# Weight maxima turned on VectorE before they go to memory, in a one-core hybrid attention layer

## The chip, the cores and the metric

The kernel runs on one core of one Trainium2 chip. The metric is the device time of one execution in microseconds (us). The core has five engines with instruction streams of their own: TensorE (PE in the profile, with PEld for its weight loads), VectorE (DVE), ScalarE (ACT), GpSimd (POOL) and SyncE (SP). SP and POOL also issue DMA transfers, each from its own queue, and all transfers share the core's 16 DMA engines.

## The reference

One decoder layer of 2048 tokens with 1024 features, depth 1. A modulated, normalised input goes through one wide projection; two mixers work on it (causal "forgetting" attention with 8 heads, and sliding-window attention with 8 query heads on 2 key heads); each mixer's output is gated, both go through one output projection, a norm and a residual.

```python
mod = jax.nn.silu(c) @ w_ada[l] + b_ada[l]
shift, scale, gate = jnp.split(mod, 3, axis=-1)
h = rms_norm(x, g_pre[l]) * (1.0 + scale[:, None, :]) + shift[:, None, :]
proj = h @ w_in[l]
qa, ka, va, fa, za, qb, kb, vb, zb = jnp.split(proj, split_points, axis=-1)
oa = forgetting_attention(qa, ka, va, fa + b_fgate[l])      # heads of 64
oa = oa * jax.nn.silu(za)
ob = sliding_window_sink_attention(rope(qb), rope(kb), vb, sinks[l])
ob = ob * jax.nn.silu(zb)
y = jnp.concatenate([oa, ob], axis=-1) @ w_out[l]
x = x + gate[:, None, :] * rms_norm(y, g_post[l])
```

## The kernel before

**Numbers in two halves.** Every large product is made of 16-bit matmuls: an operand is scaled by a power of two and split into a high and a low fp16 half, and three of the four products of halves are summed. For weights the power of two comes from the largest absolute value of a block of 128 columns (a "key": `kb`, `vb`, `qb0`-`qb3`, `zb0`-`zb3`, `va0`-`va3`, `za0`-`za3`, `qk0`-`qk7`; a `qk` key holds a head's 64 query and 64 key columns of the forgetting attention).

**How a key's weights are made ready.** For all but the first three keys, eight steps stand as events at fixed distances ahead of the key's first matmul, counted in units of projection work (42, 31, 21, 12, 8, 6, 4 and 3 units ahead):

1. `w_load` (L204): POOL issues the load of the block, 128 partitions x 8 x 128 numbers.
2. `w_max` (L210): VectorE reduces it to one largest absolute value on each partition, 128x1. Its `put` (L215) has POOL write these 128 numbers to a small tensor in memory, `mx_d` (three of them in turn). In the projection and sliding-window stage `put` follows at once; in the forgetting-attention stage it is held back for four ticks of the order (`lag`).
3. `w_back` (L225): POOL issues a read of the 512 bytes that spreads all 128 numbers over every partition (`mxr`, 128x128). It has to wait until `mx_d` has landed.
4. `w_scale` (L236 on): VectorE reduces `mxr` along the row, so that every partition knows the largest of all, and makes the power of two and its inverse in four small instructions (five for `qk` keys).
5. `w_high` (L251, ScalarE) and `w_low` (L257, VectorE, two parts) make the halves; `w_done` makes the factors for later scalings.

The keys `kb`, `vb` and `zb0` take their maxima in the first stage through TensorE instead and don't use `mx_d`.

**Stages and order.** The order of instructions is written out by hand: a list of projection units is worked off (`fill`), and between them stand the events, delayed pieces of work (`after`, `tick`) and the attention steps. In the first stage the modulation is computed and the input is normalised and turned (`hT`); then come projections mixed with rotary work (`evac_rope`: SP copies `qf` to `qs` with halves exchanged, POOL multiplies by the sines at L717, VectorE adds at L718); then, from about 140 us on, windows of the sliding attention (`Pair`) with projections between; from about 446 us the forgetting attention. `gates` (from L773) computes the logarithms of the forget gates: VectorE L782 joins them and TensorE sums them at L787 and L788.

In the forgetting attention each head's q and k come out of TensorE at L313, are split (`evac_qk`, ScalarE L1002 and VectorE L994) and copied by five SP transfers (L997 to L1000) into the tile `T`, where they stand twice in different arrangements. `max_units` (TensorE L1213, VectorE L1216 and L1218) reads `T` to find row maxima of scores. A `Step` computes scores into `sta` (L1262, L1263), exponentials (ScalarE L1267), a causal mask (POOL L1271), high and low halves (ScalarE L1275, VectorE L1278) and the product with the values (L1288, L1290, L1291) in `poa`. At the end of a row block VectorE divides (`ona`, L1295 and L1297), and the next block may use `poa` again. SP stores `ona` to memory; in the last stage the outputs are gated, turned and multiplied with the output weights (L1413).

POOL's queue holds, in order, weight loads (L204), writes and read backs of maxima, gate stores (`z_d`, L361), the rotary multiplication (L717), output stores of the sliding windows (L897), copies of sinks (L848) and the causal mask (L1271). All of them are worked off in the order in which they were issued, also when the first in line waits.

Of the kernel before, what the change touches and what calls it, by code (L numbers as in the profile page):

```python
# [10 lines left out]
F32 = mybir.dt.float32  # L11
# [4 lines left out]
ALU = mybir.AluOpType  # L16
AX = mybir.AxisListType

P = 128
# [21 lines left out]
def hybrid_layer(  # L41
# [17 lines left out]
    V, A, G, PE, SP = nc.vector, nc.scalar, nc.gpsimd, nc.tensor, nc.sync  # L59
# [12 lines left out]
    const = ctx.enter_context(tc.tile_pool(name="const", bufs=1))  # L72
# [4 lines left out]
    mx_d = [dram.tile([P, 1], F32, name=f"mx_d{n}") for n in range(3)]  # L77


    def sm(n, tag):  # L80
        return small.tile([P, n], F32, tag=tag, name=tag)
# [51 lines left out]
    cosT = swc.tile([P, S], F32, name="cosT")  # L133
    sinT = swc.tile([P, S], F32, name="sinT")
    pH = const.tile([P, 1], F32, name="pH")
    Gp = const.tile([P, KT], F32, name="Gp")
    Shp = const.tile([P, KT], F32, name="Shp")

# [46 lines left out]
    def after(n, f):  # L185
        late.append([n, f])
# [8 lines left out]
    wq = {}  # L195
    kaps_seen = []
# [9 lines left out]
        wq[key] = [raw]  # L206

    def w_max(key):
        mx = sm(1, "w_mx")
        V.tensor_reduce(mx[:], wq[key][0][:], axis=AX.XY, op=ALU.max, apply_absolute_value=True)  # L210
        md = mx_d[len(kaps_seen) % 3]
        kaps_seen.append(key)

        def put():
            G.dma_start(md[:], mx[:])  # L215
            wq[key].append(md)

        if lag[0]:
            after(lag[0], put)
        else:  # L220
            put()
# [684 lines left out]
    def add(key, us):  # L906
        if key not in pkeys and key not in ("kb", "vb"):
            at = len(punits) - (24 if key[:2] == "za" else 0)
            for n, (lead, f) in enumerate(((42, lambda: w_load(key, pieces(key))), (31, lambda: w_max(key)),
                                           (21, lambda: w_back(key)), (12, lambda: w_scale(key)),  # L910
                                           (8, lambda: w_high(key)), (6, lambda: w_low(key, 0)),
                                           (4, lambda: w_low(key, 1)), (3, lambda: w_done(key)))):
                if key == "zb0":
                    if n >= 3:
                        events.setdefault(n + 9, []).append(f)
                else:
                    events.setdefault(max(at - lead, n), []).append(f)
        if key not in pkeys:
            pkeys.append(key)
        punits.extend(us)  # L920
# [3 lines left out]
    for kind, j in (("zb", 0), ("zb", 1), ("va", 0), ("zb", 2), ("zb", 3), ("va", 1), ("va", 2)):  # L924
        key = f"{kind}{j}"
# [549 lines left out]
    with tc.manual_schedule():  # L1475
# [28 lines left out]
        for s, stp_ in enumerate(steps):  # L1504
            hd, r = divmod(s, NS)
# [100 lines left out]
```

## Time and profile before

| | |
|---|---|
| median of 3 runs | 1215.64 us (1214.23 to 1216.64) |
| profiled execution | 1216.32 us; its span, first to last instruction, 1214.5 us |
| mean granted TensorE clock | 0.982 |
| TensorE busy | 1159.6 us (95%), 10704 matmuls |
| VectorE busy | 909.5 us (75%), 2267 instructions |
| ScalarE busy | 673.4 us (55%) |
| GpSimd (POOL) busy | 175.0 us (14%), 315 instructions |
| DMA | 120.70 MB, mean 99 GB/s over the span |

Busy time of TensorE counts matmuls whose ends are modelled, since they are pipelined: in a run of matmuls of 512 columns a new one starts about every 0.216 us although each is shown as 0.38 us long. A row of the order of time names start, length, engine, line, operation, output and inputs, how many instructions were merged, and in brackets how long the engine had been idle and what ended that. A row of waits has who waited at which line, for whom, then the us in total, how many times, and the longest. A row of DMA issues ends with the KB of one transfer and the median us from issue to landing.

### The profile page before, as it was taken

The page shows a single profiled execution, that of the slowest core. Times are in us where ns is not written, and L with a number is a line of the kernel's source. Part 1 is how long each engine was busy: PE and PEld are TensorE (multiplying, and loading weights), DVE is VectorE, ACT ScalarE, POOL GpSimd, SP SyncE. Part 2 cuts the span into 40 slices and gives each one's busy share as a digit, 9 for nine tenths or more (in the row PEclk, how much of TensorE's full clock was granted, in tenths as well). Part 3 has the DMA queues.
Part 4 walks back from the last instruction along what each step waited for, and adds up shares of the span by engine and source line. Part 5 has one row for each costly group of instructions (what it writes and reads, how often), then busy time and mean ns, then how long its engine had stood idle before and what let it go on. Part 6 is the DMA issues. An engine that isn't in the chain of part 4 may idle for free. (4 is left out here: it accounts for less than half of the span.)

```text
span 1214.5 us, 27231 instructions
## 1 busy us (share of the span) xinstructions
PE 1159.6 (95%) x10704; PEld 690.9 (57%) x10704; DVE 909.5 (75%) x2267; ACT 673.4 (55%) x1116; POOL 175.0 (14%) x315
## 2 busy tenths in 40 slices
PE   5889999999999999999999999999999979999997
PEld 2467545865558975555555555555555545555553
DVE  6776567686866646788988799878978797666665
ACT  2766436555555451466666666666766788333231
POOL 2011122223232210111111121111000000000000
PEclk9799999999999999999999999999999999999999
DMA  9554333323323322242324332222111135445652
GB/s 323 189 144 143 83 81 82 90 56 102 91 68 91 56 48 58 73 92 58 67 75 58 93 82 73 44 72 48 38 47 43 58 117 189 144 157 191 199 168 84
DMA packets 88036, 120.70 MB, mean 99 GB/s; under 512 B 27836, under 2 KB 63716, under 8 KB 87908
## 3 DMA queue, kind: packets, MB, share of 16 engines
q1 hardware_dynamic: 76932, 85.94, 23.8%
q0 software_dynamic: 10976, 33.03, 11.9%
q8 instruction: 84, 1.38, 0.6%
q14 instruction: 44, 0.36, 0.2%
HBM read 71.56 MB, written 25.18 MB: 80 GB/s over the span
## 5 line engine op out<-in xcount | busy, mean ns | idle before, releaser
L1267 ACT ACTIVATE p<-sta,lift,scl_qk 128x1024 f32<-128x1024 f32 (+2 forms) x160 | 171.7, 1073 | 113.6 <-PE sta L1263 102.4
L313 PE MATMUL bk<-hT,wh_qk 128*128 128x512 f16 x768 | 196.4, 382 | 0.0
L1413 PE MATMUL bk<-wohl,oz 128*128 128x512 f16 x768 | 172.4, 379 | 2.2 <-DVE oz L1400 1.0
L1278 DVE TENSOR_TENSOR pha<-p,pha 128x1024 f16<-128x1024 f32 (+2 forms) x160 | 170.0, 1063 | 0.2 <-ACT pha L1275 0.2
L1275 ACT ACTIVATE pha<-p 128x1024 f16<-128x1024 f32 (+2 forms) x160 | 148.1, 926 | 37.0 <-POOL p L1271 29.7
L1216 DVE TENSOR_REDUCE a_m<-bk 128x1 f32<-128x512 f32 x192 | 130.0, 686 | 45.8 <-PE bk L1213 45.5
L1413 PEld LDWEIGHTS <-oz 128*128 128x128 f16 x768 | 74.4, 99 | 84.2 <-issue 1.8
L1288 PE MATMUL poa<-vt,pha 128*128 128x65 f16 x1088 | 117.6, 194 | 3.3 <-DVE ona L1297 3.3
L1291 PE MATMUL poa<-vt,pha 128*128 128x65 f16 x1088 | 117.1, 193 | 1.6 <-DVE pha L1278 1.6
L1290 PE MATMUL poa<-vt,pha 128*128 128x64 f16 x1088 | 117.5, 196 | 0.0
L313 PEld LDWEIGHTS <-wh_qk 128*128 128x128 f16 x768 | 72.9, 98 | 75.9 <-issue 2.8
L1262 PE MATMUL sta<-T 128*128 128x512 f16 (+1 forms) x320 | 110.3, 350 | 5.6 <-ACT p L1267 5.5
L1288 PEld LDWEIGHTS <-pha 128*128 128x128 f16 x1088 | 102.1, 97 | 18.1 <-DVE ona L1297 4.6
L1213 PE MATMUL bk<-T 66*128 66x512 f16 (+2 forms) x320 | 110.0, 350 | 2.5 <-DMA T<-stq 2.4
L1290 PEld LDWEIGHTS <-pha 128*128 128x128 f16 x1088 | 101.6, 97 | 13.4
L1263 PE MATMUL sta<-T 69*128 69x512 f16 (+1 forms) x320 | 108.5, 349 | 0.0
L1291 PEld LDWEIGHTS <-pha 128*128 128x128 f16 x1088 | 101.4, 99 | 2.0 <-DVE pha L1278 2.0
L313 PE MATMUL bk<-hT,wh_za 128*128 128x512 f16 x384 | 99.9, 379 | 0.0
L331 PE MATMUL bk<-wh_va,hT 128*128 128x128 f16 x1536 | 91.0, 220 | 1.4 <-issue 1.4
L1271 POOL TENSOR_SCALAR_AFFINE_SELECT p<-p 128x256 f32<-128x256 f32 x64 | 32.6, 509 | 414.2 <-ACT p L1267 409.4
L331 PEld LDWEIGHTS <-hT 128*128 128x128 f16 x1536 | 87.4, 98 | 6.5 <-issue 3.9
L313 PE MATMUL bk<-hT,wh_zb 128*128 128x512 f16 x384 | 89.7, 380 | 0.0
(487 smaller groups left out, 1941.7 us busy)
## 6 DMA issues: line engine op xcount, KB each, us to landing
wa<-in_w_ada_dram SPq DMA_DIRECT2D x16, 512.0 KB
z_d<-tz POOLq DMA_DIRECT2D x32, 256.0 KB, 2.7
T<-stq SPq DMA_DIRECT2D x128, 64.0 KB
T<-o_d SPq DMA_DIRECT2D x16, 512.0 KB
T<-z_d SPq DMA_DIRECT2D x16, 512.0 KB
xr<-in_x_dram SPq DMA_DIRECT2D x16, 512.0 KB
out_dram<-yg SPq DMA_DIRECT2D x15, 512.0 KB
xt<-in_x_dram SPq DMA_DIRECT2D x12, 512.0 KB
```

Source lines behind the costliest of these rows:

```text
L313: PE.matmul(ps, whl[:, a, k, :], hT[ci][:, b, k, :], start=(k == 0 and n == 0), stop=(k == KT - 1 and n == 2))
L331: PE.matmul(ps[:, u * P:(u + 1) * P], hT[ci][:, a, k, u * P:(u + 1) * P], whl[:, b, k, :], start=(k == 0 and n == 0), stop=(k == KT - 1 an ...
L1213: PE.matmul(mx[:, :w], T[0:XM, 0, i * P:(i + 1) * P], T[0:XM, 2, pc * CH:pc * CH + w], start=True, stop=True)
L1216: V.tensor_reduce(m3[:, u, pc:pc + 1], mx[:, :w], axis=AX.X, op=ALU.max)
L1262: PE.matmul(self.st[:, o:o + w], T[:, 3, kb_], T[:, 1, qc], start=True, stop=False)
L1267: A.activation(self.p32[:, :self.w], self.st[:, :self.w], AF.Exp, scale=scl[f"qk{self.hd}"][:], bias=lift[:])
L1275: A.activation(self.ph[:, 0, :self.w], self.p32[:, :self.w], AF.Copy)
L1278: V.tensor_tensor(self.ph[:, 1, :self.w], self.p32[:, :self.w], self.ph[:, 0, :self.w], op=ALU.subtract)
L1288: PE.matmul(po[:, u, :], ph[:, 0, pq], vt[:, b, hd, 0:65], start=(self.first and n == 0 and u == 0), stop=False)
L1290: PE.matmul(po[:, u, 0:64], ph[:, 0, pq], vt[:, b, hd, 65:VW], start=False, stop=False)
L1291: PE.matmul(po[:, u, :], ph[:, 1, pq], vt[:, b, hd, 0:65], start=False, stop=(self.last and n == len(self.blocks) - 1))
L1413: PE.matmul(py, self.hl[:, i, k, :], w_slot(8 * j + k)[:, cc], start=(k == 0 and m_ == 0), stop=(k == KT - 1 and m_ == 2))
```

## The change

`w_max` no longer leaves its 128 maxima in a tile of one column. They go into the first column of a tile `wmx` of 32 columns (the rest was set to zero once, by a memset at the start), and VectorE turns that tile in blocks of 32x32 into one of three tiles `wmt`. Of each block of 32 partitions the first row then holds 32 maxima side by side. `put` writes these four rows, on partitions 0, 32, 64 and 96, to `mx_d`: four pieces of 128 bytes where there were 128 pieces of 4 bytes. The bytes in `mx_d` and all that reads them are as before, and 23 keys go this way.

```diff
+    wmx = const.tile([P, 32], F32, name="wmx")
+    wmt = [const.tile([P, 32], F32, name=f"wmt{n}") for n in range(3)]
+    V.memset(wmx[:], 0.0)
...
     def w_max(key):
-        mx = sm(1, "w_mx")
-        V.tensor_reduce(mx[:], wq[key][0][:], axis=AX.XY, op=ALU.max, apply_absolute_value=True)
-        md = mx_d[len(kaps_seen) % 3]
+        V.tensor_reduce(wmx[:, 0:1], wq[key][0][:], axis=AX.XY, op=ALU.max, apply_absolute_value=True)
+        md, mt = mx_d[len(kaps_seen) % 3], wmt[len(kaps_seen) % 3]
+        V.transpose(mt[:], wmx[:])
         kaps_seen.append(key)
 
         def put():
-            G.dma_start(md[:], mx[:])
+            G.dma_start(md[:].rearrange("(b j) o -> b (j o)", b=4),
+                    mt[:].rearrange("(b r) j -> b r j", b=4)[:, 0, :])
             wq[key].append(md)
```

## The prediction

> **What bounds the kernel now.** I read the page's busy times first, then the waits of TensorE by stage, then the order of time around each wait that a weight maximum could touch.
>
> ```profile
> PE 1159.6 (95%) x10704; PEld 690.9 (57%) x10704; DVE 909.5 (75%) x2267; ACT 673.4 (55%) x1116; POOL 175.0 (14%) x315
> mx_d<-w_mx POOLq DMA_DIRECT2D x23, 0.5 KB, 8.5
> mxr<-mx_d POOLq DMA_DIRECT2D x23, 64.0 KB, 4.8
> z_d<-tz POOLq DMA_DIRECT2D x32, 256.0 KB, 2.7
> ...
> L215 POOL DMA_DIRECT2D mx_d<-w_mx x23: 538/562/758, 118.1 to 839.1; - x23
> ...
> POOL mxr L225 <- DMA mx_d<-w_mx: 73.6, 14, 8.8
> SPq L1000 <- DMA T<-stq: 3.0, 1, 3.0
> ...
> PE bk L1213 <- DMA T<-stq: 2.4, 1, 2.4
> ...
> PE bk L331 <- issue: 1.4, 1, 1.4
> PE bk L787 <- DVE nf L782: 1.3, 1, 1.3
> PE bk L1162 <- DVE vt L340: 1.1, 1, 1.1
> ...
> PE poa L1288 <- DVE ona L1297: 0.7, 1, 0.7
> ```
>
> TensorE is busy 95% of the span, so a change on POOL or VectorE can pay only where TensorE stands idle. The last group of rows are its waits from 100 to 480 us and, the very last, the longest from 480 to 900 us; the 23 weight maxima are all written between 118 and 840 us (the row of L215), so these few waits are all there is to win. The DMA rows hold the oddity: the 512 bytes of a maximum (128 partitions, one 4-byte number each) take 8.5 us to land, while 256 KB of a gate tile take 2.7 us from the same queue. POOL waits for that landing 14 times, 73.6 us together, before it can issue the read back. At 14% busy POOL is not the bound; the 73.6 us are worth only what TensorE loses through them.
>
> Two of TensorE's waits lead back to that landing. The first is the 1.3 us at L787 (order of time, lines that are not on the path left out):
>
> ```profile
> 135.49 0.54 POOL L215 DMA_DIRECT2D mx_d<-w_mx  x1 [6.01 <-DVE w_mx L210]
> 137.23 1.27 POOL L717 TENSOR_TENSOR qs<-qs,sinT 128x512 f32<-128x512 f32 x1 [1.20 <-DMA qs<-qf]
> 143.06 5.34 PE L313 MATMUL bk<-hT,wh_zb 128*128 128x512 f16 x24
> 143.38 0.58 POOL L225 DMA_DIRECT2D mxr<-mx_d  x1 [4.88 <-DMA mx_d<-w_mx]
> 143.93 0.69 DVE L708 SCALAR_TENSOR_TENSOR qc<-bk,cosT 128x512 f32<-128x512 f32 x1 [2.28 <-ACT qf L703]
> 145.41 0.31 ACT L779 ACTIVATE na<-na 128x128 f32<-128x128 f32 x1
> 148.30 0.28 DVE L236 TENSOR_REDUCE w_mx<-mxr 128x1 f32<-128x128 f32 x1 [3.67 <-DMA mxr<-mx_d]
> 149.26 0.28 DVE L782 SCALAR_TENSOR_TENSOR nf<-nf,na 128x128 f32<-128x128 f32 x1
> 149.69 0.46 PE L787 MATMUL bk<-nf,triu 128*128 128x128 f32 x2 [1.29 <-DVE nf L782]
> ```
>
> Write issued at 135.49, read back at 143.38, landed at 148.30, where VectorE had stood 3.67 us. L782, which TensorE needs, is queued behind that on VectorE although its own input was ready at 145.72. Twenty-four matmuls in 5.34 us, the last of them 0.38 long, start every 0.216 us; the next could have started at 143.06 + 24 x 0.216 = 148.24. The gap is 149.69 - 148.24 = 1.45 us.
>
> The second is the 2.4 us at L1213, the first matmul that reads the new q and k of head 0:
>
> ```profile
> 456.55 0.63 SPq L999 DMA_DIRECT2D T<-stq  x1
> 456.65 6.64 PE L313 MATMUL bk<-hT,wh_qk 128*128 128x512 f16 x30
> 456.74 0.58 POOL L215 DMA_DIRECT2D mx_d<-w_mx  x1 [10.64 <-DVE w_mx L210]
> 457.85 0.55 POOL L215 DMA_DIRECT2D mx_d<-w_mx  x1 [0.53 <-DVE w_mx L210]
> 465.63 0.48 SPq L1000 DMA_DIRECT2D T<-stq  x1
> 465.70 0.22 PE L1213 MATMUL bk<-T 66*128 66x128 f16 x1 [2.42 <-DMA T<-stq]
> 465.98 1.09 POOL L225 DMA_DIRECT2D mxr<-mx_d  x2 [7.57 <-DMA mx_d<-w_mx]
> ...
> 459.00:460.00 1.00, 1.00 (x6) 0.48 (x5) 0.00 (x0) 0.56 (x1) 0.00 (x0) 1.00 0.07 10
> 464.00:465.00 1.00, 0.00 (x0) 0.00 (x0) 0.00 (x0) 0.00 (x0) 0.00 (x0) 1.00 0.15 32
> ```
>
> TensorE and the SP queue both wait for copies into T and both go on at 465.6 to 465.7, within 0.4 us of the landing of the two maxima written at 456.74 and 457.85. In between the DMA engines move next to nothing: the last two columns of the stretches at 459 and 464 us are a DMA share of 0.07 and 0.15 and 10 and 32 GB/s. Copies that are neither moving nor landed are held by something, and what is in flight is the two writes of 4-byte pieces. I read it so: the pieces hold the engines that T's copies also need. That is an inference from coincidence in time, the weakest step here. Thirty matmuls end at 463.29, the last start is 462.91, the next could come at 463.13: a gap of 465.70 - 463.13 = 2.57 us.
>
> **The change, part by part.**
>
> *The write as four pieces.* 23 writes stay 23 writes, by the same queue, of the same 512 bytes; 128 pieces of 4 bytes become four of 128 bytes. No row shows such a write. Below stands the 2.7 us of the gate tile, whose 128 rows are far longer; above the 8.5 us of today. Spread evenly over the 16 DMA engines, today's 128 pieces are eight an engine, so that a piece costs about (8.5 - 2.7) / 8 = 0.7 us; one piece an engine gives 3.4 us, four on one engine 2.7 + 4 x 0.7 = 5.6 us. I take 3 us, nearest to the gate row, since four pieces leave almost nothing to queue up; 2.7 and 8.5 remain as ends.
>
> What that does at 148 us: the write lands at 138.5, just as POOL comes out of L717 (137.23 + 1.27 = 138.50), which stands between write and read back in its queue. Read back at 138.5, landed 4.9 later (148.30 - 143.38) at 143.4. VectorE reaches L236 after L708, at 144.6; from L236 to L782 are 149.26 - 148.30 = 0.96 us, so L782 runs at 145.7 and ends at 146.0, before 148.24. The gap closes whole, by 1.45 us, and does so for any landing up to 8.5 - 2.2 = 6.3 us. What is late next there: nothing on TensorE until the weights of the next z key, whose VectorE work moves up with the same chain.
>
> At 463 us: without the two slow writes the copy issued at 456.55 has 463.13 - 456.55 = 6.6 us before TensorE wants it. I take all 2.57 us as won. Today each engine carries sixteen pieces of the two writes, and the copies come free 465.63 - 456.74 = 8.9 us after the first; if one engine took all eight pieces of the new writes at the same price, half of that, 4.5 us, would set the copies free at 461.2, still before 463.13. From here to the end TensorE is the bound but for the gaps shown, so both gains carry through.
>
> The other 12 of POOL's 14 waits, and all the earlier read backs, are worth nothing: TensorE has no wait listed beside them. The 1.4 us at L331 and the 1.1 us at L1162 end on VectorE and ScalarE work ordered behind SWA windows, not on a maximum.
>
> *The transpose on VectorE.* 23 new instructions of 128x32, each needing the reduce just before it. Nearest rows, the pair of maxima whose delay TensorE does feel (its wait of 0.7 us at L1288), and the maxima and busy times (third number of the last row: VectorE) from 480 to 900 us:
>
> ```profile
> 150.79 0.09 DVE L794 MEMSET na<- 128x32 f32 x1
> 150.87 0.33 DVE L795 COPY na<-cm 128x32 f32<-128x32 f32 x1
> 151.68 0.18 DVE L800 TENSOR_TENSOR tot<-na,cm 128x24 f32<-128x24 f32 x1
> ...
> 569.06 1.21 DVE L210 TENSOR_REDUCE w_mx<-wr_qk 128x1 f32<-128x1024 f32 x1
> 570.19 1.21 DVE L210 TENSOR_REDUCE w_mx<-wr_za 128x1 f32<-128x1024 f32 x1
> 573.12 0.42 DVE L1297 TENSOR_TENSOR ona<-poa,a_ri 128x256 f32<-128x256 f32 x1
> ...
> 573.60 0.21 PE L1288 MATMUL poa<-vt,pha 128*128 128x65 f16 x1 [0.70 <-DVE ona L1297]
> ...
> L210 DVE TENSOR_REDUCE w_mx<-wr_qk x6: 1209/1212/1217, 504.4 to 834.3; 128x1 f32<-128x1024 f32 x6
> L210 DVE TENSOR_REDUCE w_mx<-wr_za x3: 1209/1212/1214, 570.2 to 835.4; 128x1 f32<-128x1024 f32 x3
> ...
> 480.00:900.00 420.00, 418.58 (x4094) 235.01 (x4092) 356.17 (x800) 271.98 (x315) 58.53 (x101) 1.00 0.28 66
> ```
>
> The bounds for its duration are 0.09 (a memset reads nothing) and 0.33 us; I take 0.18, of the two-operand row nearest in size. To this comes a lost overlap: today the next instruction starts 1.13 us after a reduce of 1.21, and a dependent one can't, which adds 0.08 plus about 0.03 of hand-over; the next instruction regains some 0.04. So about 0.25 us a maximum (0.1 to 0.45), 23 x 0.25 = 5.8 us of VectorE in all. Most of it lies in VectorE's idle time or behind TensorE. Behind a new transpose stand the scores' maxima, the low halves and L1297 of the attention; only at 573 us does TensorE wait for that queue, and the two maxima ahead of it cost 0.5 us there (0.2 to 0.9).
>
> *The write waits for the transpose* instead of the reduce: 0.25 us later on POOL, inside POOL's own idle time.
>
> *The memset of wmx* sits first on VectorE at the start, ahead of the memset for whose end the first loads wait: 0.09 us, which I charge at 0.1. Three more small tiles add no instruction.
>
> A rule of the Trainium skill speaks against the four pieces: its page "DMA: Bandwidth & Descriptors", section "Specifications", says that pieces below 512 bytes make the DMA do read-modify-write, and the section "Rules for kernel authors" that an outer dimension of four confines a transfer to at most four engines. Taken strictly, 128 bytes are as slow a size as 4, and a piece of 32 times the bytes may hold its engine longer than my 0.7 us; then the first gap still closes and the second may not, and the sum would be that of the first rival below instead of -3.4. No run here shows a 128-byte write yet, so the rule counts in that rival's chance. The same rules section says that a strided last dimension becomes one descriptor per element, with which the 8.5 us against 2.7 agree.
>
> **The sum**, against the profiled execution's 1216.32 us (span 1214.5): -1.45 - 2.57 + 0.5 + 0.1 = -3.4 us, 1212.9. That execution lies 0.7 above the median of 1215.64, so I state the change from the median: 1212.2 us.
>
> **Rivals.**
> - *Only the first gap closes.* T's copies are held by something else than the maxima, or a 128-byte piece holds its engine far longer than a 4-byte one, over (463.13 - 456.74) / 8 = 0.8 us for eight on one. For it: the coincidence is all the evidence. Against it: the SP queue's wait of 3.0 us for such a copy occurs once in the whole trace, here, where two maxima fly together. -1.45 + 0.6 = -0.85: 1214.8.
> - *The change doesn't shorten the landing.* If a short write to memory is slow whatever its form, both gaps stay and the transposes remain: +0.6, 1216.2. Against it: the gate tile's 2.7 us by the same queue.
> - *Slower: VectorE becomes the bound of the attention sweep.* Nine maxima, six of q and k and three of za, lie between 480 and 900 us, where VectorE is busy 356 of 420 us. If every one reaches TensorE at 0.25 to 0.3 us, that is 2.6 instead of 0.5 us; without the gains it gives +2.7, 1218.3. With both gains kept, it decides only where a maximum costs over 0.7 us (4.0 + 2.4 over nine). Against it: between 480 and 900 us TensorE's list shows but one wait of this kind.
> - *More than forecast.* POOL's shorter queue also pulls in the 1.4 us at L331: 1210.8. Nothing in the order of time shows the link.
>
> **How the numbers follow.** Forecast 0.58, only one gap 0.16, nothing shortened 0.10, slower 0.06, more 0.10. A difference of 0.2% is 2.4 us, about what a measurement here can tell from none, so the line is 1213.2. The forecast's own range is 1211.0 to 1213.4 (copies still held for part of the time, 0.2 to 0.9 at 573 us), of which I put 0.08 above the line. Faster: 0.50 + 0.10 = 0.60; same: 0.08 + 0.16 + 0.10 = 0.34; slower 0.06. The range takes in the forecast, more, and one gap: 1210.4 to 1215.6.
>
> **What would show it.** mx_d's time to landing near 3 us instead of 8.5; TensorE's waits at L787 and at L1213 gone; SP's 3.0 us at L1000 gone; POOL's 73.6 us down to some 15; 23 new VectorE instructions near 0.18 us; TensorE's wait at L1288 near 573 us grown to about 1.2. I am wrong if mx_d lands late all the same, if L1213 waits for T with no small write in flight, or if L1288's waits multiply.

## Result, and the profile after

The kernel after takes 1208.81 us (median of 6 runs, 1206.35 to 1210.0), 0.9939 of the kernel before (95% interval 0.9924 to 0.9955). Run again twice beside later experiments it stood at 0.9945 (0.9928 to 0.9961) and 0.9935 (0.9920 to 0.9950). The change made it faster by some 7 us, about twice the 3.4 us of the forecast; 1208.81 lies below the range. The profiled execution took 1208.93 us, its span 1207.2.

The busy times of the page after:

```profile
PE 1157.2 (96%) x10704; PEld 690.0 (57%) x10704; DVE 913.0 (76%) x2291; ACT 673.9 (56%) x1116; POOL 176.4 (15%) x315
```

The DMA issues after (KB of one, median us to landing):

```profile
mxr<-mx_d POOLq DMA_DIRECT2D x23, 64.0 KB, 3.3
mx_d<-wmt POOLq DMA_DIRECT2D x23, 0.5 KB, 1.7
```

The tile `wmt` (duration in ns, least, median and most; then who waited for it):

```profile
L214 DVE STREAM_TRANSPOSE wmt<-wmx x23: 211/211/213, 118.1 to 830.1; 128x32 f32<-128x32 f32 x23
...
  POOL mxr L229: 5.4, 6
```

The landing fell from 8.5 to 1.7 us, further than the 3 us assumed; POOL's wait for it fell from 73.6 to 5.4 us; the read back lands in 3.3 instead of 4.8 us. A transpose takes 0.21 us, for an assumed 0.18.

TensorE's waits after, from 100 to 480 us, and then the longest from 480 to 900 us:

```profile
PE px L406 <- DVE xt L400: 1.7, 4, 0.8
PE bk L1166 <- DVE vt L344: 1.1, 1, 1.1
PE bk L1166 <- DVE sc_h L112: 0.2, 1, 0.2
...
PE poa L1292 <- DVE ona L1301: 1.3, 1, 1.3
```

Against the list of before, four waits are gone: L787 (1.3), L1213 (2.4), L331 (1.4), which the forecast had left standing, and 0.4 us at L889, a row that the prediction's list left out. L1288, now L1292, has grown from 0.7 to 1.3 us.

Laid side by side, the two kernels' 10704 matmuls come in the same order, so the offset between their start times shows where time was won. It moves by +0.3 us up to 149 us, -1.45 at L787, -0.24 and -0.61 at two matmuls of L889 (200 and 318 us), -1.55 at L331, -1.7 in eight equal steps from 448 to 451 us, -2.58 at L1213, +0.59 at L1288 (573 us), +0.29 at L1291 (706 us) and -0.3 behind 1000 us: -7.25 us together, for spans that differ by 7.3.

The chain at the first gap after, in order of time (lines that are not on the path left out):

```profile
138.76 0.58 POOL L229 DMA_DIRECT2D mxr<-mx_d  x1
143.38 5.34 PE L317 MATMUL bk<-hT,wh_zb 128*128 128x512 f16 x24
144.87 0.27 DVE L240 TENSOR_REDUCE w_mx<-mxr 128x1 f32<-128x128 f32 x1
146.08 0.29 DVE L786 SCALAR_TENSOR_TENSOR nf<-nf,na 128x128 f32<-128x128 f32 x1 [0.17 <-ACT na L783]
148.56 0.38 PE L791 MATMUL bk<-nf,triu 128*128 128x128 f32 x2
```

This is the working of the forecast to 0.4 us, of which TensorE's offset of 0.3 up to here is most: read back at 138.5 forecast and 138.76 measured, VectorE at 144.6 and 144.87, L782 (now L786) at 145.7 and 146.08. In its last step L786 waits 0.17 us for ScalarE (L783) and no longer for the chain of the weights.

The wait that was not forecast, TensorE's order of time before:

```profile
423.18 6.37 PE L331 MATMUL bk<-wh_va,hT 128*128 128x128 f16 x111
430.94 0.66 PE L331 MATMUL bk<-wh_va,hT 128*128 128x128 f16 x9 [1.38 <-issue]
```

And the same 120 matmuls after:

```profile
421.11 6.87 PE L335 MATMUL bk<-wh_va,hT 128*128 128x128 f16 x120
```

Nothing ended the 1.38 us before: "issue" is time in which the engine waited for nothing that the profile shows. Counted in order, 384 matmuls of this line a key, the stopped ones are the last nine that use va2, whose halves were ready at 400.7 us; va3's first matmul comes at 433.04. So the instructions themselves are suspected. They come by DMA too, in the rows named "instruction". The DMA view before over the 9.8 us from 419.7, in which the maximum of `qk0` was being written (packets, MB, share of 16 engines):

```profile
q8 instruction: 2, 0.03, 3.8%
q14 instruction: 2, 0.02, 3.1%
```

And after, from 417.8 us, where the same write stands:

```profile
q8 instruction: 2, 0.03, 1.6%
q14 instruction: 2, 0.02, 0.9%
```

Of 9.8 x 16 = 157 engine-us, 3.8% are 6.0 us for two loads, 3.0 us each in the mean, where after it is 2.5 us, 1.25 each.

### The profile page after: what moved, and what is told of

Read it like the earlier page. It is cut to its first block, busy times and chain, and to the rows that moved or that the text cites. A ratio compares the mean times of both kernels' runs of the same rounds, so it can differ in the third digit from the quotient of the medians.

```text
span 1207.2 us, 27261 instructions
## 1 busy us (share of the span) xinstructions
PE 1157.2 (96%) x10704; PEld 690.0 (57%) x10704; DVE 913.0 (76%) x2291; ACT 673.9 (56%) x1116; POOL 176.4 (15%) x315
## 3 DMA queue, kind: packets, MB, share of 16 engines
q8 instruction: 84, 1.38, 0.5%
## 5 line engine op out<-in xcount | busy, mean ns | idle before, releaser
L317 PE MATMUL bk<-hT,wh_qk 128*128 128x512 f16 x768 | 194.6, 378 | 0.0
L1292 PE MATMUL poa<-vt,pha 128*128 128x65 f16 x1088 | 117.2, 193 | 3.9 <-DVE ona L1301 3.9
L1292 PEld LDWEIGHTS <-pha 128*128 128x128 f16 x1088 | 101.8, 97 | 18.9 <-DVE ona L1301 5.2
L1217 PE MATMUL bk<-T 66*128 66x512 f16 (+2 forms) x320 | 109.8, 350 | 0.1
```

The source lines that it names most:

```text
L317: PE.matmul(ps, whl[:, a, k, :], hT[ci][:, b, k, :], start=(k == 0 and n == 0), stop=(k == KT - 1 and n == 2))
L1217: PE.matmul(mx[:, :w], T[0:XM, 0, i * P:(i + 1) * P], T[0:XM, 2, pc * CH:pc * CH + w], start=True, stop=True)
L1292: PE.matmul(po[:, u, :], ph[:, 0, pq], vt[:, b, hd, 0:65], start=(self.first and n == 0 and u == 0), stop=False)
```

## The experiments

Theory H (holding): the 4-byte pieces hold the DMA engines for some 8 us, and whatever else wants them waits: T's copies, read backs, instruction loads. Theory R (read back): only a maximum's own chain counts, write, landing, read back, scale. All kernels are compared with the kernel before, run beside them.

**One key at a time.** The form of the write is chosen by key:

```diff
+    NEW = ("qk0",)     # or ("va3",), ("qk1", "za0"), ("zb1",)
...
+        if key in NEW:
+            V.tensor_reduce(wmx[:, 0:1], ...)
+            V.transpose(mt[:], wmx[:])
+        else:
+            V.tensor_reduce(mx[:], ...)        # and G.dma_start(md[:], mx[:]), as before
```

> The kernel before, with the new form (turned, four pieces) for the maximum of the weights qk0 alone; the 22 others keep 128 pieces of 4 bytes. In the kernel before this maximum is written at 419.68 us and TensorE stands idle for 1.4 us until 430.94 us at L331, released by nothing that the trace shows, in the middle of a run of matmuls whose weights (va3) are ready.
> Theory H (holding): the 4-byte pieces hold the DMA engines for 8 to 9 us for whatever else wants them, among it the loading of TensorE's own instructions. The write of qk0 lies over 419.7 to 428.3 us, so the wait at L331 goes with it: 1.55 us of TensorE's time won, the waits at L787 (1.3) and L1213 (2.4) stay; about 1214.2 us.
> Theory R (read back): only the chain of a key's own weights counts, write, read back, scale, split. The matmuls at 430.94 use va3, not qk0, so the wait at L331 stays at 1.4 us: 1215.7 us, with 0.1 to 0.2 us for the new memset in both cases. The stretch at half clock around 448 us (8 matmuls 0.21 us later each, 1.7 us) may or may not be there.

> The kernel before, with the new form for the maximum of the weights va3 alone, written at 403.44 us in the kernel before; its read back was issued after 4.7 us of waiting, and the matmuls at L331 that stop for 1.4 us at 429.6 us use just these weights.
> Theory R (read back): the weights of va3 come 7 us earlier into scale and split, POOL is free earlier, and the wait at L331 goes: 1.4 to 1.55 us won, about 1214.2 us.
> Theory H (holding): the maximum of qk0 is still written in 4-byte pieces at 419.7 us and still holds the engines until 428.3 us, so the wait at L331 stays at 1.4 us: 1215.7 us. L787 and L1213 stay under both.

TensorE's waits with qk0 alone changed (L801, L1227 and L903 are L787, L1213 and L889 of before):

```profile
PE bk L1227 <- DMA T<-stq: 1.6, 1, 1.6
PE pob L903 <- DVE ptb L889: 1.5, 1, 1.5
...
PE bk L801 <- DVE nf L796: 0.2, 1, 0.2
```

And with va3 alone changed (L345 is L331):

```profile
PE bk L1227 <- DMA T<-stq: 2.0, 1, 2.0
...
PE bk L327 <- DVE wh_zb L271: 1.1, 1, 1.1
PE bk L345 <- issue: 0.9, 1, 0.9
PE bk L801 <- DVE nf L796: 0.7, 1, 0.7
```

With qk0 in four pieces the wait on issue is gone (ratio 0.9975, 0.9962 to 0.9987); with va3 0.9 us of it stay (0.9993, 0.9982 to 1.0004). The expectations take the stopped matmuls for va3's; they are va2's, so that only_va3 is no test of theory R, and what counts is that the wait goes with qk0's write, on whose weights no matmul here depends. The other waits change from one execution to the next: L787 stands at 0.2 and 0.7 us here without its key having been touched.

> The kernel before, with the new form for the two maxima qk1 and za0 alone (written at 456.74 and 457.85 us in the kernel before).
> Theory H: the copies into T issued from 456.55 us on are no longer held, and TensorE's wait of 2.4 us at L1213 goes, worth 2.57 us; SP's wait of 3.0 us at L1000 goes with it. The waits at L787 (1.3) and L331 (1.4) stay: about 1213.2 us.
> Rival: T's copies are late for a reason of their own (their number, or the queue of SP), the wait at L1213 stays above 1.5 us and the time within 1 us of 1215.7.

> The kernel before, with the new form for the maximum of zb1 alone (written at 135.49 us in the kernel before). This isolates the forecast's first gap.
> The prediction's chain (write, read back, VectorE behind the read back): TensorE's wait at L787, 1.3 us in the kernel before, goes whole, and so does the 1.1 us at L313 behind wh_zb that some kernels with a short-piece zb1 show; the waits at L331 and L1213 stay near 1.4 and 2.4 us: 1.3 to 1.5 us faster than the kernel before.
> Rival: it was another transfer, held by these pieces or by others, that ended last there, and a wait at L787 of 0.5 us or more remains.

The pair: the wait at L1213 gone, L331 (1.7) and L787 (2.8) there; 0.9961 (0.9943 to 0.9979). zb1: the wait at L787 gone, a wait of 2.7 at L1213 and 1.1 on issue at L331 there; 0.9991 (0.9977 to 1.0004). So both gaps of the forecast hang on the maxima that it named, though zb1's gain can't be told from none in the times. The profiles of all versions agree: the wait at L1213 is there in all five with the pair in 128 pieces (before, only_qk0, only_va3, only_zb1, turn_only: 1.6 to 3.2 us), the one at L331 in all five with qk0 in 128 pieces (before, only_va3, only_pair, only_zb1, turn_only: 0.9 to 1.7). Neither is in any kernel that writes these maxima in four pieces and adds no 4-byte write beside them.

**The transposes alone.**

```diff
+        V.tensor_reduce(mx[:, 0:1], ...)      # mx: one of three cleared tiles of 32 columns
+        V.transpose(mt[:], mx[:])             # read by nothing
...
+            G.dma_start(md[:], mx[:, 0:1])    # 128 pieces of 4 bytes
```

> The kernel before with the 23 transposes on VectorE added and their results used by nothing: each maximum is reduced into column 0 of one of three cleared tiles, turned, and written from column 0 in 128 pieces of 4 bytes as before.
> This measures the price alone: 0.2 us a transpose, felt at 573 us (0.6), at 706 us (0.3) and at the start (0.3 for three memsets): 1.2 us slower than the kernel before in the order of time, not to be told from no change in the medians; mx_d lands in 8 to 9 us as before and the waits at L331 and L1213 stay, near 1.4 and 2.4 us.
> Rival: the transposes themselves shift VectorE enough to remove one of those waits; then the change's gain would not be the form of the write.

1.0012 (0.9997 to 1.0027): no gain. All three waits stay, 1.1 us at L787, 1.6 on issue at L331 and 3.2 at L1213, with 1.0 more on issue at L870; in TensorE's offset 0.44 us come at 573 us and 0.19 at 706 us. The gain is the write's.

**Held engines without a chain.** The kernel after, and behind each new write one more that nobody reads:

```diff
+            G.dma_start(ex_d[kaps_seen.index(key)][:], ones[:, 0:1])
```

> The kernel after, with one more write behind each of the 23 new ones, from the same queue: 128 pieces of 4 bytes of a constant into a piece of memory of its own that nobody reads. No chain of weights waits for it; it only occupies DMA engines.
> Theory H (holding): the waits that the change removed come back, though every maximum is written in four pieces: TensorE's 2.4 us at L1213 (T's copies held) and the 1.4 us at L331 behind qk0, and in part the 1.3 us at L787, since the read back is held behind the extra pieces: 1213 to 1217 us.
> Theory R (read back): the maxima themselves still land in about 1.6 us, none of the three waits comes back, and the 23 issues of 0.6 us on POOL cost nothing: 1208.8 to 1209.5 us.

Landings:

```profile
mxr<-mx_d POOLq DMA_DIRECT2D x23, 64.0 KB, 8.9
mx_d<-wmt POOLq DMA_DIRECT2D x23, 0.5 KB, 1.7
ex_d<-ones POOLq DMA_DIRECT2D x23, 0.5 KB, 7.8
```

TensorE's waits (L895, L1219 and L337 are L889, L1213 and L331 of before):

```profile
PE pob L895 <- DVE ptb L881: 5.7, 4, 2.5
PE bk L1219 <- DMA T<-stq: 5.4, 1, 5.4
PE pob L895 <- issue: 3.4, 2, 2.1
...
PE bk L337 <- issue: 1.4, 2, 1.1
```

1234.23 us, 1.0133 (1.0114 to 1.0152): 25 us above the kernel after, more than theory H had said and beyond what the change had won. The maxima land in 1.7 us as after; T's copies are late and TensorE waits on issue all the same, and the read backs are late too: 8.9 us instead of 3.3. Before, POOL stood waiting for the landing before it issued a read back, which kept the 64 KB out of the held time; here it is issued into it, and VectorE waits up to 6.9 us for it. That the windows at L895 are late for this reason is read from the order of the queues; no run separates it from other late copies. In TensorE's offset the waits at L895, L1219 and L337 make some 17 of the 25 us, and after its idle stretches the granted clock is 0.50 for 13.7 us between 420.9 and 485.8 us, which costs about 5.5 more, an estimate from the same offset. The wait at L787 did not come back.

**How short a piece.** The same extra write with `ones[:, 0:32]` and `ones[:, 0:128]`: 128 pieces of 128 and of 512 bytes.

> The kernel after with one more write behind each of the 23 new ones, as in extra4, but of 128 pieces of 128 bytes (16 KB of a constant, into memory that nobody reads).
> If what holds the engines is the number of short pieces, whatever their bytes below some size (theory N), it lands as late as the 7.8 us of extra4's writes, the read backs take 8 to 9 us again and the time is that of extra4, 1230 us or more.
> If it is the 4 bytes of a piece (theory S: single elements are slow, and pieces of 128 bytes are not), it lands in 2 to 3 us and costs next to nothing: 1209 to 1211 us.

> The same with pieces of 512 bytes: 128 pieces, 64 KB. Theory N with a limit between 128 and 512 bytes: it lands in 2 to 4 us and costs at most 2 us in all, 1209 to 1211 us, while extra128 costs 20 us. Theory S: as extra128, 2 to 3 us and 1209 to 1211 us. If the number of pieces alone counted, it would land in 8 us as well and cost 20 us.

With 128 bytes:

```profile
ex_d<-ones POOLq DMA_DIRECT2D x23, 16.0 KB, 1.8
```

With 512 bytes:

```profile
ex_d<-ones POOLq DMA_DIRECT2D x23, 64.0 KB, 2.1
```

Ratios 0.9941 (0.9920 to 0.9961) and 0.9933 (0.9909 to 0.9958), as the kernel after, and none of the three waits. It is the 4 bytes, not the number of pieces and not 128 bytes being short; sizes between the two were not run. The Trainium skill's page "DMA: Bandwidth & Descriptors" says in its section "Specifications" that transfers below 512 bytes are read, modified and written; the runs show no price of that at 128 bytes (1.8 against 2.1 us), and only 4-byte pieces were dear.

> The kernel before with each maximum written and read back for 64 of the 128 partitions only: 64 pieces of 4 bytes. It leaves out the maxima of the other 64 rows of the weights.
> If the holding goes by the number of pieces: landing near 1.6 + (8.5 - 1.6) x 60/124 = 4.9 us; the pair at 456.7 us sets T's copies free near 461.3 us, before TensorE wants them at 463.1, so the wait at L1213 goes or falls below 0.5 us, and the one at L331 falls below 0.5 us: 1209.5 to 1212 us.
> Rival: a short write has a fixed price; it lands in 7 us or more and the waits at L331 and L1213 stay: 1215 to 1217 us.

The edit is `md[0:64], mx[0:64]` in the write; the read back is halved with it, to 32 KB, and the maxima of the other 64 rows are left out. The write landed in 6.9 us, not in 4.9, but the time was 1209.62 us, 0.9944 (0.9923 to 0.9964): no wait at L331, 1.0 us at L1213, 0.3 at L787, and 1.1 at L313 behind `wh_zb`, a wait that the kernel before doesn't have. Half the pieces, with half the read back, free the engines for most of what needs them although the last piece lands only 1.6 us sooner. What sets the landing is open; it doesn't go by the count in a straight line, and it is not the measure of the harm.

**The instruction loads.** The extra write behind qk0's maximum alone, once and then twice:

```diff
+            if key == "qk0":
+                G.dma_start(ex_d[:], ones[:, 0:1])
```

> The kernel after with one extra write in all, behind the new write of qk0's maximum near 418 us: 128 pieces of 4 bytes of a constant, into memory that nobody reads.
> Theory H, with TensorE's instruction loading as what is held: a wait of TensorE on issue at L331 (now L335), 1 to 1.7 us near 428 us, comes back, with no other of the removed waits: 1210 to 1210.5 us. The read back of qk0's maximum is late too, but its weights are not due before 444 us.
> Rival: the wait at L331 needs more than held engines (POOL's queue waiting for the landing, or the late read back); with POOL not waiting it stays away: 1208.8 to 1209.7 us, no wait on issue.

> The kernel after with two extra writes of 128 pieces of 4 bytes in a row behind qk0's new write, instead of extra_qk0's one; nobody reads them, and POOL waits for neither. In extra_qk0 the instruction load nearest to the extra write began 1.6 us behind it and was not held; with two writes the engines are held some 14 to 16 us, to about 434 us, and one or two of the loads that come every 7 us must fall into that.
> Theory H: TensorE waits on issue, 1 us or more in all, between 425 and 437 us; 1209.5 to 1212 us. Rival: without POOL waiting for a landing TensorE never waits on issue here, however long the engines are held: no such wait, 1208.7 us.

One write: no wait, 1208.71 us (0.9935, 0.9916 to 0.9954), against theory H as it was written down. Its two q8 loads took 2.0% of the same 157 engine-us, 1.6 us each; its two q14 loads took 3.3%, as long as before (3.1%), and nothing stopped. Two writes, TensorE's order of time:

```profile
419.81 5.91 PE L339 MATMUL bk<-wh_va,hT 128*128 128x128 f16 x103
430.00 1.45 PE L339 MATMUL bk<-wh_va,hT 128*128 128x128 f16 x12 [4.28 <-issue]
```

The DMA view from 418.6 to 436 us:

```profile
q14 instruction: 2, 0.02, 3.4%
q8 instruction: 1, 0.02, 0.5%
```

A wait of 4.28 us, and 1214.09 us, 0.9988 (0.9972 to 1.0003). Two loads of 8 KB took 3.4% of 278 engine-us, 9.5 us together, nearly all of it the first. TensorE was idle from 426.4 to 429.8 us, and the granted clock was 0.50 for the next 3.4 us, which adds to the wait. POOL waited for no landing and no weights were late: 4-byte writes that nobody reads stop TensorE. That a late load of instructions is the link is argued, not shown: before, the long loads were q8's, here q14's, and extra_qk0 has q14's as long as before without a wait. Which of the two instruction rows feeds which engine the traces don't say. The Trainium skill's page "DMA: Bandwidth & Descriptors" has in its section "Queues, rings and completion order" a mechanism that fits: an engine changes between queues only after a whole packet of pieces; the runs show the effect (other queues' transfers late by 2 to 9 us), not the packets.

**Versions to keep.** The transposes where they pay, and the pairs of maxima taken apart:

```diff
-            for n, (lead, f) in enumerate(((42, ...), (31, lambda: w_max(key)),
+            for n, (lead, f) in enumerate(((42, ...), (28 if key[:2] == "za" else 31, lambda: w_max(key)),
```

> The kernel after, unchanged, on the same chip as the next three, so that they have it beside them. Expected 1208.8 us, ratio 0.993 to 0.995 to the kernel before; TensorE's waits at L787 (now L791), L331 (L335) and L1213 (L1217) absent again if the 4-byte pieces caused them; its wait behind the attention's L1297 (L1301) near 566 us again about 1.3 us. Rival: the waits come and go by chance from execution to execution, and one of the three shows here too.

> The kernel after with the new form for the first 14 maxima alone (up to qk1 and za0); the nine maxima of the forgetting attention are written in 128 pieces of 4 bytes as before, without a transpose on VectorE; the memset of wmx stands behind the copy of the identity instead of first.
> Theory H (holding, and the transposes as the price): the three waits stay away, TensorE's wait near 566 us falls from 1.3 to 0.7 us, the 0.3 us near 699 us and the 0.2 us at the start go: 0.6 + 0.3 + 0.2 = 1.1 us better than the kernel after, about 1207.7 us; the pieces hold engines in the attention too, but TensorE waits for no copy there.
> Rival: holding hurts in the attention as well (a late instruction load, a late row of T), and the time is 1209 us or more, with a wait on a DMA or on issue between 500 and 850 us.

> The kernel after with one number changed: the maxima of the za weights are taken 28 instead of 31 units ahead, so that they no longer fall into the same step as a q and k maximum (two reduces and two transposes in a row, 2.9 us of VectorE).
> If the 1.3 us that TensorE waits near 566 us are the price of two maxima in a row, this wait falls to 0.3 us or less and the time by about 1 us, to 1207.8 us.
> Rival: one reduce and one transpose (1.45 us) ahead of the attention's L1301 are enough to make TensorE wait as before, or the maximum moved meets another step that can't spare it; no gain, 1208.8 us or above.

> A kernel from the findings: first14 (four pieces for the 14 maxima ahead of the forgetting attention, 128 pieces and no transpose for the nine in it, memset of wmx later) with the za maxima 28 instead of 31 units ahead, as in after_split.
> The wait of 0.7 us that first14 still has near 566 us goes, and no transpose is left there: some 0.7 us below first14's 1208.3, 1207.6 us; against the kernel after 1.0 to 2 us faster.
> Rival: the maximum that is moved meets another step that needs VectorE (after_split showed 0.6 us at L1217 for that), and the gain is given back: 1208.3 us.

first14: 1208.30 us (0.9933, 0.9916 to 0.9950), -0.59 at 566 us and -0.29 at 699 us against the kernel after, as expected. after_split: 1208.61 (0.9935, 0.9918 to 0.9952), TensorE's wait near 566 us gone (-1.45), 0.72 given back at L1217. Neither can be told from the kernel after beside them (1209.72 us; 0.9945, 0.9928 to 0.9961). Both together, "best", lost everything: 1216.35 us, 0.9997 (0.9984 to 1.0011). POOL's order of time there:

```profile
570.85 0.56 POOL L228 DMA_DIRECT2D mx_d<-w_mx  x1
571.40 0.54 POOL L238 DMA_DIRECT2D mxr<-mx_d  x1
580.01 0.54 POOL L238 DMA_DIRECT2D mxr<-mx_d  x1 [8.07 <-DMA mx_d<-w_mx]
580.55 0.42 POOL L1285 TENSOR_SCALAR_AFFINE_SELECT p<-p 128x256 f32<-128x256 f32 x1
```

ScalarE's longest wait from 570 to 584 us, and TensorE's from 560 to 600:

```profile
ACT pha L1289 <- POOL p L1285: 7.9, 2, 7.7
...
PE sta L1276 <- ACT p L1281: 4.3, 1, 4.3
```

Moved three units later, the 4-byte write is issued only at 570.85 us, behind a causal mask (first14: 563.75, ahead of it), and its landing is waited for ahead of the next mask: POOL waits 8.1 us for it, the mask L1285 is queued behind that wait, ScalarE waits 7.7 us for the mask and TensorE 4.3 for ScalarE. That is half of the loss. From 578.1 to 581.5 us TensorE was busy 7%, and the granted clock was 0.50 for the next 6.8 us, which costs some 2.6 us in its offset; 1.2 us more come at L1276 near 851 us, where POOL again waits for two landings. This is the price of POOL's wait that the prediction looked for and found nowhere; a shift of three units makes it.

> after_split (four pieces everywhere, the za maxima 28 instead of 31 units ahead) with the memset of wmx behind the copy of the identity: the last of the better versions. Expected 1208.0 us, 1 to 1.5 us below the kernel after; rival: no difference that the medians can tell.

> The kernel after, unchanged, beside split2 and extra_qk0: 1208.8 to 1209.7 us, none of the waits at L787, L331 and L1213 (in its own lines L791, L335, L1217).

split2 1207.48 us (0.9927, 0.9911 to 0.9942) beside 1208.43 for the kernel after (0.9935, 0.9920 to 0.9950): ahead in the medians, not told apart by the intervals. It is the best median of all versions. Its trace has TensorE's wait at L1292 near 566 us gone, and 0.6 us at L1217 in its place, as after_split.

## Why the prediction was wrong

**Right.** Where the two gaps come from: zb1's maximum (-1.45 forecast and measured, chain to 0.4 us) and the copies of T held by the pair (-2.57 forecast, -2.58 measured). "What is in flight is the two writes of 4-byte pieces", called there the weakest step, held: only_pair takes the wait away, extra4 brings it back without any chain. The transposes' price at 573 us was 0.59 for a forecast 0.5, with 0.29 more at 706 us, where the forecast had charged nothing; from the first reduce of the pair to the second are 1.49 us after, where the forecast reckoned 1.13 + 0.25.

**Wrong: the step that stopped at two and put the rest at nothing.** "The other 12 of POOL's 14 waits, and all the earlier read backs, are worth nothing" and "the 1.4 us at L331 and the 1.1 us at L1162 end on VectorE and ScalarE work ... not on a maximum". The row of L331 says "issue", not VectorE. The prediction had just inferred that the pieces hold the engines from T's copies, and did not ask what else goes through these engines: instruction loads, the suspected link at L331 (-1.55), and other SP copies. The -0.85 at the two matmuls of L889 came with late VectorE work. The 0.61 at 318 us fits: all six profiled versions that write the maxima of 284 and 294 us in 128 pieces wait there, the kernel before among them (0.3 to 1.5 us). The 0.24 at 200 us stood behind the rotary copies `qs`, which POOL got at 194.6 us, 9 us into the write of 185.6; turn_only, only_pair and the other versions that keep that write in 128 pieces don't have it, so it comes and goes. The rival "More than forecast" had the place and no link, "POOL's shorter queue"; extra2_qk0, where TensorE stops and POOL waits for no landing, shows that this link isn't needed. That rival stood at 0.10.

**Mis-sized: a landing of 3 us.** It was 1.7. The price of 0.7 us a piece was taken over to pieces of 128 bytes; extra128 shows 128 of those landing in 1.8 us. The rule weighed there, that 128 bytes are as slow a size as 4, was wrong for this case. No term of the sum hung on it: both gaps close with 3 us as with 1.7.

**No term at all: the clock.** 1.7 us of the profiled difference are the eight matmuls from 448 us, each 0.21 us later. The two stretches in question before (length, busy times, granted clock, DMA):

```profile
444.57:447.98 3.41, 1.91 (x13) 1.04 (x11) 2.76 (x15) 3.39 (x10) 0.71 (x1) 1.00 0.14 43
447.98:451.40 3.42, 3.42 (x9) 1.22 (x8) 0.00 (x0) 3.42 (x8) 0.00 (x0) 0.50 0.00 0
```

And after:

```profile
441.49:444.91 3.42, 2.35 (x13) 1.33 (x14) 2.31 (x14) 3.42 (x8) 0.71 (x1) 1.00 0.12 38
444.91:448.32 3.41, 3.41 (x18) 1.47 (x15) 0.00 (x0) 3.41 (x8) 0.00 (x0) 1.00 0.00 0
```

Between the sliding windows and the attention TensorE idles for some 1.5 us in both kernels. Before, it was busy for 56% of one stretch of 3.41 us, and the granted clock was 0.50 for the whole next one; after, the same idle time fell across a boundary (69% busy) and no halving followed. only_qk0, only_va3 and extra512 show the halving (56% busy each), the last with every maximum in four pieces; only_pair, only_zb1, turn_only and the kernel after's two repeats don't. So it comes and goes with either form, and these 1.7 us of the pair of executions can't be booked as a gain of the change. The Trainium skill's page "TensorE: Matmul & The Clock Gate" says in its section "Part 1: The HAM clock gate" that such windows run free of the kernel's start, which fits. How much idle time halves the clock stays open: a stretch near 430 us in only_pair, 51% busy, was followed by full clock, while 0.50 followed stretches that were 0% busy (extra2_qk0), 7% (best) and 31% (only_pair, behind its wait of 2.8 us at L787). Over all runs the clock is not quite indifferent to the change: the mean granted clock is 0.984 in 85 runs of the kernel before and 0.986 in 18 of the kernel after, 2.7 us less of lost clock. Among the 85 a lost us goes with 0.3 us of time, so an estimate of its worth is 0.8 us; whether the removed waits are its cause was not tested.

**The other rivals.** "Only the first gap closes" fell with the wait at L1213, "doesn't shorten the landing" with the 1.7 us. "VectorE becomes the bound" fell too: 0.59 and 0.29 us at two of its places, not at nine. All that the prediction listed as signs of being right came; the wait on issue at L331, which was not on the list, went too.

## What to carry to other kernels

When a few tiny pieces are seen to delay one transfer, list everything that shares the engines, read backs and instruction loads included, before writing that the rest is worth nothing; a wait of TensorE on "issue" in the middle of a run of ready matmuls is then a suspect. A write of one number per partition is worth a transpose of 0.2 us where something waits for what it holds up; in the attention stage the transposes could not be told from the 4-byte writes (first14). Wherever 4-byte writes must stay, look at what the issuing queue holds behind the wait for their landing, since a shift of a few units turned a free wait into a loss of 8 us here.

## What the hardware showed

- 128 pieces of 4 bytes land in about 8 us and hold other queues' transfers meanwhile; 128 pieces of 128 bytes land in 1.8, 128 of 512 bytes in 2.1, four of 128 bytes in 1.7 us.
- 64 pieces of 4 bytes still land only after 6.9 us, but do little harm.
- With two 4-byte writes in a row, two instruction loads took 9.5 us together and TensorE stopped for 4.28 us with no semaphore in sight.
- After a wait of some us the granted clock can be halved for the next 3.4 or 6.8 us, so that the wait costs more than its length (extra2_qk0, best, extra4).
- The waits that 4-byte writes cause vary from execution to execution (L787: 0.2 to 2.8 us with zb1 written in 4-byte pieces).
